# Output projection of a hybrid block by one level of Strassen's algorithm, with later left factors and accumulating transfers

## The chip, the cores and the metric

The kernel runs on one core of a Trainium2 chip, in one launch. The time is that of one execution on the device, in microseconds (us). The core has TensorE for matrix products (PE in the profile, PEld for its weight loads), VectorE (DVE), ScalarE (ACT), GpSimd (POOL) and SyncE (SP). Sixteen DMA engines carry the transfers of all queues; SP's queue for loads and POOL's software queue (q0 in the profile) matter here.

## The reference

The input `x` is 512 frames of 1024 features in float32. A layer normalises it, projects it with `w_in`, runs three branches (gated linear attention, forgetting attention, attention to memory tokens), and merges them. The part that the change touches comes after the branches:

```python
merged = gt[:, :, 0] * y_gla + gt[:, :, 1] * y_fox + gt[:, :, 2] * y_mem
h = h + merged @ w_out[l]                      # output projection, 512 x 1024 by 1024 x 1024

u2 = rmsnorm(h, g_ffn[l])
h = h + jnp.square(jax.nn.relu(u2 @ w_ff1[l])) @ w_ff2[l]    # MLP, 1024 -> 4096 -> 1024
return rmsnorm(h, g_final)
```

## The kernel before

**Matrix products.** Operands are split into a high and a low part, and each product is three matmuls (`mm3`, L159 to 162): high by high, then the two mixed ones. Weights arrive in chunks of 128 x 1024 numbers (512 KB): SP loads a chunk into `raw` (three buffers), ACT makes the high part (`whi`, L151), VectorE the low part (`wlo`, L152), with three buffers each. A chunk feeds 12 matmuls of 512 columns (24 of 256 in the MLP's first product).

**Branches and merge.** `branch` runs one of the three gated branches over eight tiles of features (`acc`, 128 features by 512 tokens). In the last branch each finished tile is halved and split into `mh` and `ml`, the left factors of the output projection.

**Output projection.** Two runs of four chunks, one per half of the output columns. Each run makes all four token tiles, `res_evac` adds a finished tile to the residual `hN[t]` (`h` in the profile) and squares it; after the second run it makes the normalised tile `un`. The second run has buffers of its own (`fhi`, `flo`) and takes the token tiles in the order 2, 3, 0, 1. `u2_turn(t)` transposes `un` of a tile on TensorE (L877) and makes the left factors of the MLP's first product for it; the turns of tiles 2, 3 and 0 are woven into the run, the turn of tile 1 follows two half products of the MLP.

**The MLP.** The 4096 hidden features are taken in four quarters `q`. In each, both products (`ff1`, `ff2`) use one level of Strassen's algorithm: an operand is cut into 2 x 2 blocks, seven products of blocks replace eight, and the factors and results are sums and differences of blocks. Left factors of `ff2` are made in `ff1_evac` behind products 7 and 3 of `ff1`. In `ff2`, products 1 and 5 stay in PSUM over the quarters, 6 and 7 are collected in `R6` and `R7`, and `evac` adds all to `hN` with VectorE; in the last quarter one of three corrections goes by an accumulating transfer from POOL (L1038).

**The sums of weights.** The right factors of the Strassen products that are sums of blocks (`T1` to `T4` for `F`, which is `w_ff1`, and `B`, which is `w_ff2`, in each quarter) are made in DRAM: a copy of one block, then transfers that add another block to it, 1 MB each. `sum_ops` lists these 64 transfers, and `next_sum` issues one on POOL's queue after each chunk's ACT cast, from the ninth cast on (`SUM_FROM = 8`). L143 is a copy, L141 an accumulating transfer.

**What sets the order.** TensorE runs in the order in which the program is written. The instructions of other engines are put in order by a scheduler ahead of time; each engine then runs its list in that order, and POOL's transfers leave through one queue in theirs.

Of the kernel before, what the change touches and what calls it, by code (L numbers as in the profile page):

```python
# [17 lines left out]
P = 128  # L18
D = 1024
# [13 lines left out]
def chunk_list():  # L33

    L = []
    L += [("T", "w_mem_kv", P * j) for j in range(4)]
    L += [("N", "w_mem_kv", 2 * j, 512) for j in range(4)]
    L += [("G",)]
    L += [("T", "w_in", OFF["fq"]), ("T", "w_in", OFF["fk"])]
    L += [("N", "w_in", 2 * j, OFF["fv"]) for j in range(4)]  # L40
    for j in range(1, 4):
        L += [("T", "w_in", OFF["fq"] + P * j), ("T", "w_in", OFF["fk"] + P * j)]
    for n, c in (("gk", 2), ("gq", 2)):
        L += [("T", "w_in", OFF[n] + P * j) for j in range(c)]
# [12 lines left out]
    return L  # L57
# [3 lines left out]
def hybrid_block(ctx, tc, chunks, wst, xT, memT, xN, cols, gffn, gfin, wup, cst, out):  # L61
# [43 lines left out]
    def load_w(key, eng=None):  # L105
# [6 lines left out]

    tsum = {(kind, n, q): dram.tile([2, P, 1024], F32, name=f"T{kind}{n}_{q}") for kind in "FB" for n in (1, 2, 3, 4)
            for q in range(4)}

# [16 lines left out]
    chunk_n = [0]  # L132
# [454 lines left out]
    def branch(gate, wo, oh, ol, n, last=None):  # L587
# [6 lines left out]
        for j in range(KT):  # L594
# [239 lines left out]
    with pool("outp") as op_:  # L834
        mh = op_.tile([P, KT, S], F32R, name="mh")
        ml = op_.tile([P, KT, S], F32R, name="ml")
        for t in range(NT):
            nc.sync.dma_start(hN[t], xN[t * P:(t + 1) * P, :])
        run(branch("gate_gla", "w_gla_o", ogh, ogl, 2, last=(mh, ml)))
        mst.close()  # L840
        oqst = ExitStack()
        oq = oqst.enter_context(pool("outq"))

        def res_evac(c):
            def go(t, ps):
                cs = slice(512 * c, 512 * c + 512)
                nc.vector.tensor_tensor(hN[t][:, cs], hN[t][:, cs], ps, op=ALU.add)
                sumsq(oq.tile([P, 512], F32, tag="hsq", name=nm("hsq"), bufs=2), hN[t], t, c, c)
                if c == 1:
                    r = rms_tile(oq, t)  # L850
                    un[t] = oq.tile([P, D], F32, tag="un", name=nm("un"), bufs=2)
                    for g in range(2):
                        gs_ = slice(512 * g, 512 * g + 512)
                        nc.vector.scalar_tensor_tensor(un[t][:, gs_], hN[t][:, gs_], r, gf[:, gs_], op0=ALU.mult, op1=ALU.mult)
            return go

        un = {}

        def own_w(key):
            hi, lo = (oq.tile([P, 1024], F32R, tag=g, name=nm(g), bufs=4) for g in ("fhi", "flo"))  # L860
            split(hi, lo, load_w(key))
            return hi, lo
# [45 lines left out]
        def load_b(kind, q, n, i):  # L908
            load_n[0] += 1
            own = kind == "B" and load_n[0] % 4 == 0  # L910
            raw = (yp if own else wp).tile([P, 1024], F32, tag="raw", name=nm("raw"))
# [10 lines left out]

        run(islice(c1, 16))
# [19 lines left out]
    with pool("ff") as yp:  # L943
# [20 lines left out]
        def ff1_evac(n, i, ps):  # L964
# [12 lines left out]
            if n == 7:  # L977
# [37 lines left out]

        def C(i, j, t):
            return hN[2 * i + t][:, 512 * j:512 * j + 512]

        def add(to, x, op=ALU.add):
            nc.vector.tensor_tensor(to, to, x, op=op)  # L1020
# [34 lines left out]
        def ff2(q):  # L1055
            for n in (1, 4, 5, 6, 7, 2, 3):
                keep = n in (1, 5)
# [24 lines left out]
def layout(inputs):  # L1082
# [7 lines left out]
    for i, c in enumerate(chunks):  # L1090
        if c[0] == "T":
            wst[i] = W[c[1]][:, c[2]:c[2] + P].reshape(KT, P, P).transpose(1, 0, 2).reshape(P, -1)
        elif c[0] == "N":
            wst[i] = W[c[1]][c[2] * P:(c[2] + 2) * P, c[3]:c[3] + 512].reshape(2, P, 512).transpose(1, 0, 2).reshape(P, -1)
        elif c[0] == "B":
            _, q, h, (kh, ch) = c
            j = 8 * q + 4 * h + int(kh) - 1
            cs = slice(512 * (int(ch) - 1), 512 * int(ch))
            for n in range(2):
                wst[i, :, 512 * n:512 * n + 512] = W["w_ff2"][(j + 2 * n) * P:(j + 2 * n + 1) * P, cs]  # L1100
        elif c[0] == "F":
# [65 lines left out]
```

## Time and profile before

| | |
|---|---|
| median of 3 runs | 865.1 us (864.47 to 867.61) |
| the profiled execution | 863.14 us, its span 861.4 us |
| PE busy | 834.2 us, 97% of the span |
| DVE / ACT / POOL busy | 558.4 / 440.1 / 95.5 us |
| output projection begins (PE) | 476.40 us |
| second product of the MLP begins (PE) | 533.70 us |

Rows of the timeline give the start in us, the duration in us, engine, line, operation, the tiles as out<-in, their shapes, how many instructions the row groups, and in brackets the idle time of the engine ahead of the row with what ended it. `mm` and `a` are PSUM tiles. In rows of groups the two numbers behind the bar are the busy time in us and the mean of one in ns. Rows by window give the length and then for PE, PEld, DVE, ACT and POOL the busy time and number, the granted clock, the share of the DMA engines and GB/s. Rows of transfers give the KB of each and the us from issue to landing. Rows of queues give packets, MB and the share of the 16 engines' time.

### The profile page before, as it was taken

How to read it: one execution, taken by the hardware profiler on the slowest of the kernel's cores; microseconds unless marked ns; L12 is line 12 of the kernel's file. 1: busy time of each engine (PE TensorE's matmuls, PEld its weight loads, DVE VectorE, ACT ScalarE, POOL GpSimd, SP SyncE). 2: the span in 40 equal slices, each digit the busy share in tenths (PEclk: the TensorE clock that was granted, in tenths of full speed). 3: DMA queues.
4: the chain of work that ended last, by engine and by line, in shares of the span. 5: the costliest groups of instructions: out<-in, count | busy, mean ns of one | idle time of the engine just before them, and what ended most of it. 6: DMA issues, size and time to landing. Idle time of an engine off the chain costs nothing. (4 is left out here: it accounts for less than half of the span.)

```text
span 861.4 us, 12076 instructions
## 1 busy us (share of the span) xinstructions
PE 834.2 (97%) x4609; PEld 711.7 (83%) x4609; DVE 558.4 (65%) x886; ACT 440.1 (51%) x704; POOL 95.5 (11%) x124
## 2 busy tenths in 40 slices
PE   7999999999999999999999998999999999999994
PEld 5778788888888888787888878997998899789973
DVE  6783756756444546474543358697579749965997
ACT  8764746754323432321332245685468448636843
POOL 5100011000101022322323200000000000000001
PEclk9999999999999999999999999999999999999998
DMA  8447789967959866699899933555554655565553
GB/s 322 143 159 255 282 204 221 215 253 188 283 192 243 315 220 186 149 221 278 294 251 342 252 128 123 172 171 196 196 174 158 218 185 175 180 208 179 172 170 117
DMA packets 39306, 180.66 MB, mean 210 GB/s; under 512 B 5040, under 2 KB 5840, under 8 KB 34640
## 3 DMA queue, kind: packets, MB, share of 16 engines
q1 hardware_dynamic: 31536, 109.09, 35.8%
q0 software_dynamic: 5920, 67.64, 30.9%
q10 hardware_dynamic: 1792, 3.16, 1.1%
q8 instruction: 36, 0.59, 0.3%
q14 instruction: 22, 0.18, 0.1%
HBM read 177.23 MB, written 69.22 MB: 286 GB/s over the span
## 5 line engine op out<-in xcount | busy, mean ns | idle before, releaser
L152 DVE TENSOR_TENSOR wlo<-raw,whi 128x1024 fp32r<-128x1024 f32 x186 | 231.8, 1248 | 163.3 <-ACT whi L151 162.8
L151 ACT CAST whi<-raw 128x1024 fp32r<-128x1024 f32 x186 | 195.3, 1051 | 240.5 <-PE mm L161 140.7
L160 PE MATMUL mm<-uhi,whi 128*128 128x512 f32 x360 | 142.5, 396 | 0.0
L161 PE MATMUL mm<-ulo,whi 128*128 128x512 f32 x360 | 140.7, 391 | 1.4 <-DVE ulo L213 1.4
L162 PE MATMUL mm<-uhi,wlo 128*128 128x512 f32 x360 | 140.5, 390 | 0.0
L161 PEld LDWEIGHTS mm<-ulo,whi 128*128 128x128 f32 x360 | 67.7, 188 | 15.7 <-DVE ulo L213 2.9
L162 PEld LDWEIGHTS mm<-uhi,wlo 128*128 128x128 f32 x360 | 67.6, 188 | 14.6 <-DVE wlo L152 0.4
L160 PEld LDWEIGHTS mm<-uhi,whi 128*128 128x128 f32 x360 | 67.7, 188 | 13.5 <-issue 0.7
L160 PE MATMUL mm<-u2h,whi 128*128 128x256 f32 x256 | 73.5, 287 | 1.5 <-ACT p L969 1.5
L162 PE MATMUL mm<-u2h,wlo 128*128 128x256 f32 x256 | 73.1, 286 | 0.0
L161 PE MATMUL mm<-u2l,whi 128*128 128x256 f32 x256 | 73.1, 286 | 0.0
L161 PE MATMUL mm<-wlo,ch 128*128 128x512 f32 x160 | 62.5, 391 | 0.7 <-DVE wlo L152 0.7
L162 PE MATMUL mm<-whi,cl 128*128 128x512 f32 x160 | 62.3, 389 | 0.0
L160 PE MATMUL mm<-whi,ch 128*128 128x512 f32 x160 | 62.3, 389 | 0.0
L161 PE MATMUL mm<-u2sl,whi 128*128 128x256 f32 x192 | 54.4, 283 | 0.0
L162 PE MATMUL mm<-u2sh,wlo 128*128 128x256 f32 x192 | 54.4, 283 | 0.0
L160 PE MATMUL mm<-u2sh,whi 128*128 128x256 f32 x192 | 54.3, 283 | 0.0
L160 PEld LDWEIGHTS mm<-u2h,whi 128*128 128x128 f32 x256 | 49.8, 195 | 1.9 <-ACT p L969 1.8
L161 PEld LDWEIGHTS mm<-u2l,whi 128*128 128x128 f32 x256 | 49.9, 195 | 0.1
L162 PEld LDWEIGHTS mm<-u2h,wlo 128*128 128x128 f32 x256 | 49.8, 195 | 0.0
L160 PEld LDWEIGHTS mm<-u2sh,whi 128*128 128x128 f32 x192 | 36.9, 192 | 0.0
L161 PEld LDWEIGHTS mm<-u2sl,whi 128*128 128x128 f32 x192 | 36.9, 192 | 0.0
(325 smaller groups left out, 1670.9 us busy)
## 6 DMA issues: line engine op xcount, KB each, us to landing
raw<-in_wst_dram SPq DMA_DIRECT2D x128, 512.0 KB, 5.9
TF<-in_wst_dram POOLq DMA_DIRECT2D x16, 1024.0 KB, 11.4
TB<-in_wst_dram POOLq DMA_DIRECT2D x16, 1024.0 KB, 11.2
raw<-TF SPq DMA_DIRECT2D x32, 512.0 KB, 4.2
raw<-TB SPq DMA_DIRECT2D x32, 512.0 KB, 3.2
xr<-in_xT_dram SPq DMA_DIRECT2D x4, 512.0 KB, 8.1
nFb<-dF ACTq DMA_DIRECT2D x8, 256.0 KB, 6.4
h<-in_xN_dram SPq DMA_DIRECT2D x4, 512.0 KB, 7.9
```

The costliest lines, as they stand in the source:

```text
L151: cast = nc.scalar.copy(hi, raw)
L152: nc.vector.tensor_tensor(lo, raw, f(hi), op=ALU.subtract)
L160: nc.tensor.matmul(ps, lh, rh, start=start, stop=False)
L161: nc.tensor.matmul(ps, lh, rl, start=False, stop=False)
L162: nc.tensor.matmul(ps, ll, rh, start=False, stop=stop)
```

## The change

- **Output projection by seven products.** `w_out` is stored in blocks like a quarter of `w_ff2` (kind `W`). Products 1, 4, 5, 6, 7, 2, 3 run in this order, each of two chunks: 14 loads where 8 were. Four of the seven right factors are sums, made in DRAM as the others are.
- **Left factors.** `merged` takes `acc` tiles in pairs, forms the differences on VectorE and splits seven slots into `mh` and `ml`, during the last branch.
- **Results.** Product 1 is copied to `E` and added to `h` by two transfers of 256 KB on POOL's queue. Behind product 6, `E` and `G` are formed on VectorE, and six transfers of 256 KB add them to `h`. The other products are added by VectorE.
- **Sums of weights.** 72 transfers instead of 64, from the fifth cast on, in three parts. The last is paced by the eighth chunk of the output projection, before by the fourth.
- **End of the projection.** Tile 0 of product 3, turns 2 and 3, tile 1 of product 3, half of the MLP's first product, turn 0, its other half, turn 1.
- **Second product of the MLP.** `late` makes the left factors S2, S3, A12 and S4 one product ahead of their use. In the last quarter product 1 goes through an ACT copy and a transfer, and all six corrections go by transfers.

```diff
-    for c in range(2):
-        L += [("N", "w_out", 2 * j, 512 * c) for j in range(4)]
+    L += [("W", 0, i, b) for b in ("11", "21", "12", "22") for i in range(2)]
...
+    quarters = [("W", 0)] + [(kind, q) for q in range(4) for kind in "FB"]
+    tsum = {(kind, n, q): dram.tile([2, P, 1024], F32, name=f"T{kind}{n}_{q}") for kind, q in quarters for n in (1, 2, 3, 4)}
...
-        for qs in ((0, 1), (2, 3)):
+        for part in (quarters[:3], quarters[3:6], quarters[6:]):
             for ops in rounds:
                 for n, src, add in ops:
-                    for q in qs:
-                        for kind in "FB":
-                            yield tsum[kind, n, q], block(kind, q, src) if isinstance(src, str) else tsum[kind, src, q], add
+                    for kind, q in part:
+                        yield tsum[kind, n, q], block(kind, q, src) if isinstance(src, str) else tsum[kind, src, q], add
...
-    SUM_FROM = 8
+    SUM_FROM = 4
...
-            if last is not None:
-                h, l = last
-                nc.scalar.mul(h[:, j, :], acc[j], 0.5)
-                nc.vector.scalar_tensor_tensor(l[:, j, :], acc[j], 0.5, f(h[:, j, :]), op0=ALU.mult, op1=ALU.subtract)
+            if last is not None and j % 2:
+                last(j // 2, acc[j - 1], acc[j])
...
+        MERGED = {1: 0, 2: 1, 4: 2, 6: 3, 7: 4, 3: 5, 5: 6}
+        mh, ml = (op_.tile([P, 4, 7, 256], F32R, name=n) for n in ("mh", "ml"))
+
+        def merged(p, e, o):
+            def to(slots, src):
+                h, l = (x[:, p, slots, :].rearrange("p s t -> p (s t)") for x in (mh, ml))
+                nc.scalar.mul(h, src, 0.5)
+                nc.vector.scalar_tensor_tensor(l, src, 0.5, f(h), op0=ALU.mult, op1=ALU.subtract)
+
+            a, b = slice(0, 256), slice(256, 512)
+            to(slice(0, 1), e[:, a])
+            to(slice(1, 3), o)
+            for dst, x, y in ((o[:, b], e[:, b], o[:, b]), (e[:, b], e[:, a], e[:, b]), (e[:, a], e[:, a], o[:, b]),
+                              (o[:, a], o[:, a], e[:, a])):
+                nc.vector.tensor_tensor(dst, x, y, op=ALU.subtract)
+            to(slice(3, 5), e)
+            to(slice(5, 7), o)
...
-        def out_w(key):
-            return own_w(key) if key[2] < 4 else get_w(key)
-
-        run(gN([("N", "w_out", 2 * j, 0) for j in range(4)], of(mh, ml), NT, at_, res_evac(0)))
-        c1 = gN([("N", "w_out", 2 * j, 512) for j in range(4)], of(mh, ml), NT, mmt, res_evac(1), tail=4, get=out_w, order=(2, 3, 0, 1))
+        def C(i, j, t):
...
+        EG = [[oq.tile([P, 512], F32, name=f"{n}{t}") for t in range(2)] for n in "EG"]
...
+        def out_evac(n, t, ps):
+            if n == 1:
+                nc.scalar.copy(EG[0][t], ps)
+                nc.gpsimd.dma_start(C(0, 0, t), EG[0][t], accum_op=ALU.add)
+            if n == 4:
+                add(C(1, 0, t), ps)
+            if n == 6:
+                E, G = EG[0][t], EG[1][t]
+                add(E, ps, ALU.subtract)
+                nc.vector.tensor_tensor(G, wps[5][t], E, op=ALU.subtract)
+                for to, x in ((C(1, 0, t), E), (C(1, 1, t), G), (C(0, 1, t), G)):
+                    nc.gpsimd.dma_start(to, x, accum_op=ALU.add)
+            if n == 7:
+                add(C(1, 0, t), ps)
+                square(2 + t, 0, 0)
+                add(C(1, 1, t), ps, ALU.subtract)
+                square(2 + t, 1, 1)
+            if n == 2:
+                add(C(0, 0, t), ps)
+                square(t, 0, 0)
+            if n == 3:
+                add(C(0, 1, t), ps)
+                square(t, 1, 1)
+        wps = {}
+        def out_mm(n, steps):
+            wps[n] = [(at_ if n == 5 else mmt)() for _ in range(2)]
+            for js in steps:
+                w = {i: [x.rearrange("p (k c) -> p k c", k=2) for x in load_b("W", 0, n, i)] for i in js}
+                for t in range(2):
+                    for i in js:
+                        for k in range(2):
+                            a, b = (x[:, 2 * i + k, MERGED[n], t * P:(t + 1) * P] for x in (mh, ml))
+                            mm3(wps[n][t], a, b, w[i][0][:, k, :], w[i][1][:, k, :], i == k == 0, i == k == 1)
+                    if js[-1] == 1:
+                        out_evac(n, t, wps[n][t])
+                    yield
+        for n in (1, 4, 5, 6, 7, 2):
+            run(out_mm(n, [[0], [1]]))
+        p3 = out_mm(3, [[0, 1]])
+        next(p3)
         u2_turn(2)
-        run(islice(c1, 8))
         u2_turn(3)
-        run(c1)
+        run(p3)
+        first = [mmt([P, 2, 256]) for _ in range(2)]
+        ff1_mm(first[0], 0, 5, 0)
         u2_turn(0)
-        first = [mmt([P, 2, 256]) for _ in range(2)]
-        for i in range(2):
-            ff1_mm(first[i], 0, 5, i)
+        ff1_mm(first[1], 0, 5, 1)
         u2_turn(1)
...
                 left(i, S1, c22[i])
-                sub(p1[i], c11[i], p1[i])
-                left(i, S3, p1[i])
-                sub(c11[i], c11[i], c22[i])
-                left(i, S2, c11[i])
             if n == 3:
                 add(p5[i], ps)
                 relu2(p5[i], p5[i])
-                left(i, A12, p5[i])
-                sub(p5[i], p5[i], c11[i])
-                left(i, S4, p5[i])
+        def late(n):
+            for i in range(2):
+                if n == 6:
+                    sub(c22[i], c11[i], c22[i])
+                    left(i, S2, c22[i])
+                if n == 7:
+                    sub(p1[i], c11[i], p1[i])
+                    left(i, S3, p1[i])
+                if n == 2:
+                    left(i, A12, p5[i])
+                if n == 3:
+                    sub(p5[i], p5[i], c22[i])
+                    left(i, S4, p5[i])
...
             if n == 1:
-                add(C(0, 0, t), ps)
+                nc.scalar.copy(p4[t], ps)
+                nc.gpsimd.dma_start(C(0, 0, t), p4[t], accum_op=ALU.add)
...
-                nc.gpsimd.dma_start(C(0, 1, t), G, accum_op=ALU.add)
-                add(C(1, 0, t), E)
-                add(C(1, 1, t), G)
+                for to, x in ((C(1, 0, t), E), (C(1, 1, t), G), (C(0, 1, t), G)):
+                    nc.gpsimd.dma_start(to, x, accum_op=ALU.add)
...
-            for n in (1, 4, 5, 6, 7, 2, 3):
+            order = (1, 4, 5, 6, 7, 2, 3)
+            for at, n in enumerate(order):
+                if at >= 2 and at < 6:
+                    late(order[at + 1])
```

On POOL, from the last tiles of the merge to the end of the projection, before (`acc<-acc,th` is a tile of the merge; `TF` and `TB` are sums of `w_ff1` and `w_ff2`):

```order
L143 DMA TB_3_107<-TB_3_99 16x16384
L141 DMA TF_2_90<-in_wst_dram 128x2048
L608 TENSOR_TENSOR acc_2104<-acc_2104,th_4076 128x512
L141 DMA TB_2_106<-in_wst_dram 128x2048
L608 TENSOR_TENSOR acc_2105<-acc_2105,th_4134 128x512
L141 DMA TF_3_91<-in_wst_dram 128x2048
L141 DMA TB_3_107<-in_wst_dram 128x2048
```

And now, where L139 is the accumulating transfer and L141 the copy (`E` and `G` are the tiles of corrections; `h_3702` to `h_3705` the four token tiles):

```order
L139 DMA TB_3_109<-in_wst_dram 128x2048
L606 TENSOR_TENSOR acc_2113<-acc_2113,th_4164 128x512
L141 DMA TB_2_103<-TB_2_101 16x16384
L141 DMA TF_3_107<-TF_3_105 16x16384
L141 DMA TB_3_111<-TB_3_109 16x16384
L139 DMA TB_2_103<-in_wst_dram 128x2048
L933 DMA h_3702<-E_4199 128x512
L933 DMA h_3703<-E_4200 128x512
L139 DMA TF_3_107<-in_wst_dram 128x2048
L139 DMA TB_3_111<-in_wst_dram 128x2048
L941 DMA h_3704<-E_4199 128x512
L941 DMA h_3705<-E_4200 128x512
```

Three copies and three accumulating transfers, with two transfers of `E` among them, now follow the last tile of the merge, and the transfers of product 6 follow those; four more of `G` come behind the last row.

On VectorE in the projection, before, from the eighth weight chunk's low half on (`hss` and `ms` are sums of squares):

```order
L152 TENSOR_TENSOR wlo_4530<-raw_4527,whi_4529 128x1024
L816 TENSOR_SCALAR hss_3698<-hss_3698 128x1
L847 TENSOR_TENSOR h_3696<-h_3696,mm_4307 128x512
L821 TENSOR_SCALAR ms_4360<-hss_3698 128x1
L854 SCALAR_TENSOR_TENSOR un_4364<-h_3696,rr_4361,gf 128x512 x2
L847 TENSOR_TENSOR h_3697<-h_3697,mm_4308 128x512
```

And now, from the eighth of fourteen on:

```order
L150 TENSOR_TENSOR wlo_4355<-raw_4352,whi_4354 128x1024
L863 TENSOR_TENSOR E_4199<-E_4199,mm_4331 128x512
L150 TENSOR_TENSOR wlo_4386<-raw_4383,whi_4385 128x1024
L863 TENSOR_TENSOR E_4200<-E_4200,mm_4332 128x512
L939 TENSOR_TENSOR G_4201<-a_4291,E_4199 128x512
L939 TENSOR_TENSOR G_4202<-a_4292,E_4200 128x512
L150 TENSOR_TENSOR wlo_4404<-raw_4401,whi_4403 128x1024
L863 TENSOR_TENSOR h_3704<-h_3704,mm_4381 128x512
L150 TENSOR_TENSOR wlo_4452<-raw_4449,whi_4451 128x1024
L812 TENSOR_SCALAR hss_3706<-hss_3706 128x1
L863 TENSOR_TENSOR h_3705<-h_3705,mm_4382 128x512
L150 TENSOR_TENSOR wlo_4470<-raw_4467,whi_4469 128x1024
```

The low half of the ninth chunk (`wlo_4386`) now stands behind the subtraction from `E_4199`, which overwrites what a transfer of product 1 reads; that of the eleventh (`wlo_4452`) stands behind the add of product 7 to `h_3704`, which comes after a transfer of product 6 into the same place.

On VectorE where the MLP's second product begins in a quarter, before (`c`, `p` and `cl` are tiles of hidden features and the low parts of left factors):

```order
L152 TENSOR_TENSOR wlo_793_5161<-raw_791_5158,whi_792_5160 128x1024
L955 TENSOR_TENSOR c111_4617<-c111_4617,c221_4619 128x512
L213 TENSOR_TENSOR cl0_4628<-c110_4616,ch0_4626 128x512
L213 TENSOR_TENSOR cl1_4629<-p51_4623,ch1_4627 128x512
L955 TENSOR_TENSOR p50_4622<-p50_4622,c110_4616 128x512
L1020 TENSOR_TENSOR h2_3696<-h2_3696,mm_781_5116 128x512
L213 TENSOR_TENSOR cl1_4629<-p11_4621,ch1_4627 128x512
L152 TENSOR_TENSOR wlo_796_5179<-raw_794_5176,whi_795_5178 128x1024
```

And now:

```order
L150 TENSOR_TENSOR wlo_817_5227<-raw_815_5224,whi_816_5226 128x1024
L211 TENSOR_TENSOR cl1_4711<-p51_4705,ch1_4709 128x512
L211 TENSOR_TENSOR cl1_4711<-p11_4703,ch1_4709 128x512
L1004 TENSOR_TENSOR p50_4704<-p50_4704,c220_4700 128x512
L863 TENSOR_TENSOR h2_3704<-h2_3704,mm_805_5176 128x512
L1004 TENSOR_TENSOR c221_4701<-c111_4699,c221_4701 128x512
L150 TENSOR_TENSOR wlo_820_5245<-raw_818_5242,whi_819_5244 128x1024
```

Between these two low halves stand five operations where six were.

More of the change, by code (lines that the diff above doesn't have):

```diff
@@ L109, in load_w @@
         return raw
-    tsum = {(kind, n, q): dram.tile([2, P, 1024], F32, name=f"T{kind}{n}_{q}") for kind in "FB" for n in (1, 2, 3, 4)
-            for q in range(4)}
+    quarters = [("W", 0)] + [(kind, q) for q in range(4) for kind in "FB"]
+    tsum = {(kind, n, q): dram.tile([2, P, 1024], F32, name=f"T{kind}{n}_{q}") for kind, q in quarters for n in (1, 2, 3, 4)}
     def block(kind, q, b):
@@ L834, in hybrid_block @@
     with pool("outp") as op_:
-        mh = op_.tile([P, KT, S], F32R, name="mh")
-        ml = op_.tile([P, KT, S], F32R, name="ml")
+        MERGED = {1: 0, 2: 1, 4: 2, 6: 3, 7: 4, 3: 5, 5: 6}
[13 more added lines that the diff above has]
+            to(slice(5, 7), o)
         for t in range(NT):
             nc.sync.dma_start(hN[t], xN[t * P:(t + 1) * P, :])
-        run(branch("gate_gla", "w_gla_o", ogh, ogl, 2, last=(mh, ml)))
+        run(branch("gate_gla", "w_gla_o", ogh, ogl, 2, last=merged))
         mst.close()
@@ L842, in hybrid_block, with add, square @@
         oq = oqst.enter_context(pool("outq"))
[L844 to L855, printed above, removed]
-        un = {}
[L859 to L862, printed above, removed]
-        def out_w(key):
-            return own_w(key) if key[2] < 4 else get_w(key)
-        run(gN([("N", "w_out", 2 * j, 0) for j in range(4)], of(mh, ml), NT, at_, res_evac(0)))
-        c1 = gN([("N", "w_out", 2 * j, 512) for j in range(4)], of(mh, ml), NT, mmt, res_evac(1), tail=4, get=out_w, order=(2, 3, 0, 1))
+        un = {}
+        def C(i, j, t):
+            return hN[2 * i + t][:, 512 * j:512 * j + 512]
+        def add(to, x, op=ALU.add):
+            nc.vector.tensor_tensor(to, to, x, op=op)
+        def square(t, c, n):
+            sumsq(oq.tile([P, 512], F32, tag="hsq", name=nm("hsq"), bufs=2), hN[t], t, c, n)
+            if n == 1:
+                r = rms_tile(oq, t)
+                un[t] = oq.tile([P, D], F32, tag="un", name=nm("un"), bufs=2)
+                for g in range(2):
+                    gs_ = slice(512 * g, 512 * g + 512)
+                    nc.vector.scalar_tensor_tensor(un[t][:, gs_], hN[t][:, gs_], r, gf[:, gs_], op0=ALU.mult, op1=ALU.mult)
+        EG = [[oq.tile([P, 512], F32, name=f"{n}{t}") for t in range(2)] for n in "EG"]
         a21, s1 = (oq.tile([P, 4, 256], F32, name=n) for n in ("a21", "s1"))
@@ L909, in load_b @@
             load_n[0] += 1
-            own = kind == "B" and load_n[0] % 4 == 0
+            own = kind != "W" and load_n[0] % 4 == 0 and not (kind == "F" and q == 0)
             raw = (yp if own else wp).tile([P, 1024], F32, tag="raw", name=nm("raw"))
@@ L921, in ff1_mm @@
                     mm3(ps[:, a, :], wh[:, a, k, :], wl[:, a, k, :], uh[:, k, :], ul[:, k, :], k == 0, k == 3)
-        run(islice(c1, 16))
+        def out_evac(n, t, ps):
+            if n == 1:
+                nc.scalar.copy(EG[0][t], ps)
[36 more added lines that the diff above has]
+        next(p3)
         u2_turn(2)
-        run(islice(c1, 8))
         u2_turn(3)
-        run(c1)
+        run(p3)
+        first = [mmt([P, 2, 256]) for _ in range(2)]
+        ff1_mm(first[0], 0, 5, 0)
         u2_turn(0)
-        first = [mmt([P, 2, 256]) for _ in range(2)]
-        for i in range(2):
-            ff1_mm(first[i], 0, 5, i)
+        ff1_mm(first[1], 0, 5, 1)
         u2_turn(1)
```

8 lines of the change are left out of this document (2 added, 6 removed).

## Prediction

> **What bounds the kernel now.** I read the page's busy shares first, then the 40 slices, then the PE timeline of the output projection.
>
> ```profile
> span 861.4 us, 12076 instructions
> PE 834.2 (97%) x4609; PEld 711.7 (83%) x4609; DVE 558.4 (65%) x886; ACT 440.1 (51%) x704; POOL 95.5 (11%) x124
> PE   7999999999999999999999998999999999999994
> PEclk9999999999999999999999999999999999999998
> DMA  8447789967959866699899933555554655565553
> ```
>
> TensorE is busy 97% of the span at full clock, so matmuls are the bound nearly everywhere, and only removed matmuls or removed waits can help. The DMA engines are the other full resource: eights and nines in slices 18 to 23 (366 to 495 us), of which the last is the first half of the output projection. Its matmuls, row by row:
>
> ```profile
> 476.40 0.39 PE L160 MATMUL a<-whi,mh 128*128 128x512 f32 x1
> 476.62 0.39 PE L161 MATMUL a<-wlo,mh 128*128 128x512 f32 x1
> 510.56 1.32 PE L877 MATMUL a<-cst_s,un 128*128 128x128 f32 x8 [1.36 <-DVE un L854]
> 524.31 0.36 PE L160 MATMUL mm<-u2h,whi 128*128 128x256 f32 x1
> 530.03 0.28 PE L162 MATMUL mm<-u2h,wlo 128*128 128x256 f32 x1
> 532.66 1.29 PE L877 MATMUL a<-cst_s,un 128*128 128x128 f32 x8 [2.35 <-DVE un L854]
> 533.70 0.36 PE L160 MATMUL mm<-u2h,whi 128*128 128x256 f32 x1
> 534.98 0.41 PE L161 MATMUL mm<-u2l,whi 128*128 128x256 f32 x1
> 535.19 0.42 PE L162 MATMUL mm<-u2h,wlo 128*128 128x256 f32 x1
> ```
>
> Durations overlap in the pipeline; the price of a matmul is the step between starts: 0.225 us for 512 columns (476.40 to 476.62; 0.227 over longer stretches), and 5.72/47 = 0.12 us for 256 (48 matmuls start from 524.31 to 530.03). The projection starts at 476.40, and the second product of the MLP's first quarter at 533.70. Between them are 192 matmuls x 0.227 = 43.6 us, four turns (transposes of one token tile) of 1.03 us (532.66 to 533.70) = 4.1, 48 x 0.12 = 5.8 us of the MLP's first product, and waits of 1.4 and 2.4: 57.3 us, all accounted for. After the second wait matmuls of 256 columns step by 0.21 instead of 0.12 (534.98 to 535.19), until 537.5; that slower clock costs about 1.6 more.
>
> **The matmuls removed.** Seven products of 24 matmuls replace 192: 168. Gain 24 x 0.227 = 5.4 us. The new end order has a half product between the last turns, so both waits (3.8) and the slow stretch (1.6) can go too. If nothing is late, the projection takes 168 x 0.227 + 4.1 + 5.8 = 48.0 us and the second product starts at 524.4, against an effective 535.3: **-10.8 us**.
>
> **The added work beside it.** Six more weight chunks are split, and the left factors of the projection are formed during the merge.
>
> ```profile
> L152 DVE TENSOR_TENSOR wlo<-raw,whi 128x1024 fp32r<-128x1024 f32 x186 | 231.8, 1248 | 163.3 <-ACT whi L151 162.8
> 440.00:460.00 20.00, 20.00 (x90) 16.57 (x89) 7.09 (x7) 5.83 (x8) 4.36 (x5) 1.00 1.02 314
> ```
>
> A chunk feeds 12 matmuls = 2.72 us, and DVE needs 1.25 for its split: covered by half. In the merge (second row: length, then PE, PEld, DVE busy) DVE works 7.1 of 20 us, so the left factors (3.8 us per pair of tiles by those counts, 1.4 before) fit. Both cost 0 while transfers keep up; uncovered, a factor pair would cost 2.4. Two ACT copies of product 1 are hidden too (ACT is busy 51%). The six more loads on SP's queue go into the next part.
>
> **The transfers, which decide it.** The sums of weight quarters that the MLP uses later are built by 1 MB transfers, all on POOL's one software queue (q0), one per weight chunk cast. Before, the last of them is issued at the fourth chunk of the projection. After, there are 72, and the last goes with the eighth. Behind sums in that same queue now stand eight 256 KB accumulating transfers: two of product 1, six of product 6. VectorE waits for these.
>
> ```profile
> 466.88 0.84 POOL L141 DMA_DIRECT2D TF<-in_wst_dram  x1 [1.65 <-ACT whi L151]
> 475.00 0.83 POOL L141 DMA_DIRECT2D TB<-in_wst_dram  x1 [4.38 <-ACT whi L151]
> TF<-in_wst_dram POOLq DMA_DIRECT2D x1, 1024.0 KB, 11.4
> ...
> q0 software_dynamic: 1099, 8.09, 73.4%
> q1 hardware_dynamic: 1036, 3.79, 17.0%
> TF<-in_wst_dram POOLq DMA_DIRECT2D x4, 1024.0 KB, 11.6
> raw<-in_wst_dram SPq DMA_DIRECT2D x8, 512.0 KB, 9.7
> ...
> q0 software_dynamic: 256, 8.39, 44.9%
> ...
> TF<-in_wst_dram POOLq DMA_DIRECT2D x1, 1024.0 KB, 8.3
> ```
>
> The first row's sum is the third (issue to landing 11.4 us): it lands at 478.3. The next four rows are the DMA view of 111 to 171 us, with eight accumulates and eight loads: one accumulate takes 0.734 x 60/8 = 5.5 us of all 16 engines, one load 0.17 x 60/8 = 1.3, together 6.8. The row after them is 59 to 111, with eight plain copies: 0.449 x 52/8 = 2.9 each. Alone, an accumulate lands after 8.3 (last row). For 256 KB I take a quarter of 5.5 = 1.4; the nearest row of that size landed after 3.3, which is the other end:
>
> ```profile
> h<-c POOLq DMA_DIRECT2D x2, 256.0 KB, 3.3
> ```
>
> By the new order of POOL, the queue then is: before the sum that lands at 478.3 an accumulate stands where a copy was (+2.6: 480.9); accumulate at the second chunk (+6.8: 487.7); three copies (+8.7: 496.4); accumulate (+6.8: 503.2); the two of product 1 (+2.8: 506.0); two accumulates, beside which no load runs if PE stands (2 x 5.5: 517.0); the first of product 6 (+1.4: **518.4**), the fifth at 524.0. Ends: 514.6 with 5.5 for each accumulate and 2.5 for a copy, 528 with 3.3 for each small one and a load's 1.3 beside each copy.
>
> What waits: ideally product 7 ends at 476.4 + 10 x 2.72 = 503.6. On VectorE the add of product 7 stands behind the first of product 6's transfers, and the low half of the eleventh chunk stands behind that add; so TensorE gets it at 518.4 + 0.68 + 1.25 = 520.3. (An earlier stop, of the ninth chunk behind product 1's transfers at 506, lies inside this.) Product 2 then runs to 525.8. VectorE waits for the fifth transfer at 524.0, then adds, makes the normalised tiles and the last two low halves in its queue:
>
> ```profile
> L1020 DVE TENSOR_TENSOR h<-h,mm 128x512 f32<-128x512 f32 x24 | 15.8, 678 | 0.0
> 509.75 1.41 DVE L854 SCALAR_TENSOR_TENSOR un<-h,rr,gf 128x512 f32<-128x512 f32 x2 [0.75 <-POOL rr L822]
> ```
>
> From 525.8: add 0.68, chunk 13 1.25, small sums 0.2, tile 1.5, chunk 14 1.25 = 530.7. TensorE then has half a product tile (1.4), two turns (2.1), the other tile (2.7), half a MLP product (2.9), a turn, the other half and a turn (4.9): 544.7. That is 20.3 past the ideal 524.4, and after so long a stop I add the 1.6 of slow clock seen above: **+21.9 us** (18 to 32 by the ends).
>
> The Trainium skill, page "DMA: Bandwidth & Descriptors", section "Anatomy of one DMA — SWDGE (gpsimd) path", fits such a transfer as about 2.0 us + bytes/436e3, an estimate of 2.4 us of moving for 1 MB. By that the queue would be empty near 500 and nothing would wait. The trace's 5.5 us of all engines per accumulate disagrees; the page describes no accumulating transfer between two DRAM places, and I go by the trace.
>
> **The MLP.** Left factors of the second product are made one product ahead instead of all in the last steps of the first, so one VectorE operation fewer stands ahead of a low half there.
>
> ```profile
> 586.30 0.50 PE L161 MATMUL a<-wlo,ch 128*128 128x512 f32 x1 [0.66 <-DVE wlo L152]
> 660.00:680.00 20.00, 19.34 (x86) 15.70 (x85) 17.93 (x23) 9.21 (x11) 0.00 (x0) 1.00 0.55 186
> 740.00:760.00 20.00, 19.34 (x86) 15.69 (x85) 17.62 (x24) 9.03 (x11) 0.00 (x0) 1.00 0.58 191
> 820.00:840.00 20.00, 19.48 (x85) 15.33 (x84) 20.00 (x27) 9.14 (x10) 0.90 (x1) 1.00 0.52 165
> ```
>
> TensorE stands about 0.5 to 0.7 at each of four boundaries; one operation of 0.68 fewer ends most of it: **-2.0** (0 to -2.6). In the last quarter eight transfers replace six VectorE adds while VectorE is busy throughout (20.00); q0 is empty there, the eight at 3.3 have the length of products 7 and 2 (10.9 us), so 0 at the end of the span, within 1 either way. The sums that start four casts earlier meet loads of 9.7 us that PE, in nines there, did not feel: 0, at most one wait like the 2.35 above.
>
> **Sum.** The profiled run took 863.1. 863.1 - 10.8 + 21.9 - 2.0 = 872.2; that run is 2.0 under the median of 865.1, so **874** against the median.
>
> **Rivals.** *Hidden* (faster): the queue drains by 503.6, fifteen us sooner than I count, and no add waits; 863.1 - 10.8 - 2.0 + 2.0 = 852. It decides when the first transfer of product 6 lands before product 7's last matmul. For it: 256 KB alone took 3.3. Against it: three quarters of the engines' time went to q0 wherever accumulates ran. The Trainium skill's fit above leads here. *Partly hidden*: engines serve q0 with most of their time, loads fall behind instead, and the landing is near 510; 874 - 8 = 866, between 855 and 868. For it: loads needed 10.5 us to land in this stage while q0 had 68%, and TensorE did not wait. *Worse*: each small transfer takes 3.3 and loads share the copies, 528: 884 and up; also if VectorE, full near the ends of the MLP, then waits for transfers there.
>
> ```profile
> q0 software_dynamic: 609, 5.24, 68.2%
> raw<-in_wst_dram SPq DMA_DIRECT2D x5, 512.0 KB, 10.5
> ```
>
> **How the numbers follow.** My forecast, a stop of TensorE of some 15 to 20 us that outweighs the matmuls saved, 0.61 (its own range 868 to 884). Hidden 0.17, partly hidden 0.13, worse 0.09. About 0.5% (4.3 us, 860.8 to 869.4) can be told from no change. Hidden and a third of partly hidden are faster: 0.22; the rest of partly hidden with the low edge of the forecast is the same: 0.12; slower 0.66. The range runs from 852, through half of the hidden case, to 888; it leaves out half of hidden (0.09) and about half of worse (0.05).
>
> **What the changed profile would show.** Right: TensorE idle over 10 us between 498 and 525, ended by VectorE's low half of the ninth and eleventh chunks, VectorE before them idle for POOL's queue; sums landing up to 517; 168 matmuls in the projection; granted clock low after the stop. The four 0.66 waits before the second product shrink. Wrong: the small transfers land within 4 us of issue and TensorE's projection takes about 48 us; or the stop is at the loads (raw) rather than the adds; or the MLP's VectorE waits grow instead.

## The result and the profile after

The changed kernel takes 894.6 us (893.1 to 895.5), against 866.1 for the kernel before in the same measurement: 1.033 times as long, 95% interval 1.030 to 1.035. The forecast of slower was right; 874, and its upper end of 888, were too low.

The page of the changed kernel, the lines that answer to those of before:

```profile
span 892.7 us, 12148 instructions
PE 841.2 (94%) x4585; PEld 715.3 (80%) x4585; DVE 574.3 (64%) x916; ACT 450.7 (50%) x722; POOL 112.7 (13%) x146
PE   7999999999999999999999657699999999999994
PEclk8999999999999999999999869799999999999998
DMA  8487998787679888658999993445645655465574
```

There are 24 matmuls fewer (4585 for 4609), yet TensorE is busy 7 us longer. In slices 23 to 26 it has holes, and its granted clock is lower there (8, 6, 9 and 7 tenths); but for the clock of the first slice, the rest of both rows is as before. So nearly the whole loss is in the projection and the turns behind it. TensorE's timeline there, only the first matmul, the main waits, and the start of the MLP's second product (560.03):

```profile
478.46 0.39 PE L158 MATMUL mm<-whi,mh 128*128 128x512 f32 x1
...
494.94 0.80 PE L158 MATMUL a<-whi,mh 128*128 128x512 f32 x1 [5.18 <-ACT whi L149]
...
515.03 0.80 PE L159 MATMUL mm<-wlo,mh 128*128 128x512 f32 x1 [1.89 <-DVE wlo L150]
...
531.86 0.80 PE L159 MATMUL mm<-wlo,mh 128*128 128x512 f32 x1 [8.54 <-DVE wlo L150]
...
542.65 0.50 PE L159 MATMUL mm<-wlo,mh 128*128 128x512 f32 x1 [2.42 <-DVE wlo L150]
...
560.03 0.36 PE L158 MATMUL mm<-u2h,whi 128*128 128x256 f32 x1
...
572.85 0.58 PE L158 MATMUL mm<-u2h,whi 128*128 128x256 f32 x1 [6.83 <-ACT p L1018]
```

And before, where the fifth product of the MLP (the one after a wait for ACT's copies `p`) starts at 542.73:

```profile
542.73 0.39 PE L160 MATMUL mm<-u2h,whi 128*128 128x256 f32 x1 [1.55 <-ACT p L969]
```

From the first matmul of the projection to the fifth product it is 572.85 - 478.46 = 94.4 us, before 542.73 - 476.40 = 66.3: +28.1. I call this stretch the stage below. TensorE's busy time grew by 2.6 us in it, by 2.3 ahead of it and by 2.1 behind. What lies ahead of it is 2.1 longer, what lies behind 1.2 (892.7 - 572.85 = 319.8 for 861.4 - 542.73 = 318.7). Ahead of it the earlier sums and the added left factors are at work, but they cost next to nothing: in the first 60 us the granted clock was 0.94 here and 1.00 before, and in two of the traces below (corrections on VectorE, more work for VectorE), with the same program up to the projection and a clock of 1.00, the projection starts at 476.60 and 476.74, before at 476.40. At 0.91 it starts at up to 481.27. So stages are the better measure between traces. They have a spread too: in the run of the MLP part alone, where nothing of the stage was edited, it took 67.9 us for 66.3 before.

The waits on VectorE in the same place:

```profile
513.15 0.69 DVE L863 TENSOR_TENSOR E<-E,mm 128x512 f32<-128x512 f32 x1 [5.05 <-DMA h<-E]
513.76 1.22 DVE L150 TENSOR_TENSOR wlo<-raw,whi 128x1024 fp32r<-128x1024 f32 x1
...
529.98 0.69 DVE L863 TENSOR_TENSOR h<-h,mm 128x512 f32<-128x512 f32 x1 [11.18 <-DMA h<-E]
530.59 1.22 DVE L150 TENSOR_TENSOR wlo<-raw,whi 128x1024 fp32r<-128x1024 f32 x1
```

These are the two operations that the prediction named (the first is the subtraction from `E`), each with the low half of a chunk behind it, the ninth and the eleventh. POOL's and ACT's timelines show where the sums stood:

```profile
485.91 0.50 POOL L141 DMA_DIRECT2D TF<-TF  x1 [3.53 <-ACT whi L149]
495.17 0.49 POOL L141 DMA_DIRECT2D TB<-TB  x1 [8.76 <-ACT whi L149]
497.56 0.85 POOL L139 DMA_DIRECT2D TB<-in_wst_dram  x1 [1.90 <-ACT whi L149]
498.11 2.11 POOL L933 DMA_DIRECT2D h<-E  x2
499.47 1.61 POOL L139 DMA_DIRECT2D TF<-in_wst_dram  x1
507.14 0.81 POOL L139 DMA_DIRECT2D TB<-in_wst_dram  x1 [6.05 <-ACT whi L149]
514.14 0.87 POOL L941 DMA_DIRECT2D h<-E  x1 [6.20 <-DVE E L863]
```

```profile
493.84 1.04 ACT L149 CAST whi<-raw 128x1024 fp32r<-128x1024 f32 x1 [8.23 <-DMA raw<-TW]
```

And the DMA view of 468 to 490 us:

```profile
q0 software_dynamic: 454, 4.19, 80.7%
q1 hardware_dynamic: 536, 1.99, 23.7%
...
raw<-TW SPq DMA_DIRECT2D x4, 512.0 KB, 13.4
...
TB<-TB POOLq DMA_DIRECT2D x1, 10.3
TF<-TF POOLq DMA_DIRECT2D x1, 8.8
```

The sums hold 81% of the engines' time, a chunk needs 13.4 us to land, ACT's cast waits 8.2 us for one, and POOL's next sum waits for that cast. The loop closes: sums make chunks late, and late chunks make the last sums late. The last one is issued at 507.14, the first small transfer of product 6 behind it at 514.14, and the add runs at 529.98.

### The profile page after: what moved, and what is told of

The parts are those of the page before. It is cut to its first block, busy times and chain, and to the rows that moved or that the text cites. A ratio compares the mean times of both kernels' runs of the same rounds, so it can differ in the third digit from the quotient of the medians.

```text
span 892.7 us, 12148 instructions
## 1 busy us (share of the span) xinstructions
PE 841.2 (94%) x4585; PEld 715.3 (80%) x4585; DVE 574.3 (64%) x916; ACT 450.7 (50%) x722; POOL 112.7 (13%) x146
## 5 line engine op out<-in xcount | busy, mean ns | idle before, releaser
L150 DVE TENSOR_TENSOR wlo<-raw,whi 128x1024 fp32r<-128x1024 f32 x194 | 241.5, 1247 | 175.1 <-ACT whi L149 170.4
L149 ACT CAST whi<-raw 128x1024 fp32r<-128x1024 f32 x194 | 203.7, 1051 | 269.6 <-PE mm L159 137.8
```

The lines of the kernel that those rows point to most:

```text
L149: cast = nc.scalar.copy(hi, raw)
L150: nc.vector.tensor_tensor(lo, raw, f(hi), op=ALU.subtract)
```

## The experiments

Theory A: VectorE waits for small transfers that stand behind sums in one queue. Theory B: the sums take the DMA engines from the chunks. Theory C, later D: the end of the projection is limited by VectorE's own work, whatever the transfers do.

**No sum in the projection.** The last eight sums come later, one per three chunks, in the MLP's first quarter.

```diff
+        if paused[0]:
+            paused[0] += 1
+            if paused[0] < 17 or paused[0] % 3:
+                return
         chunk_n[0] += 1
...
+        paused[0] = 1
         wps = {}
```

(The last edit stands ahead of the projection's first chunk.)

> The changed kernel, but no weight chunk of the projection paces a sum: the last eight sums come later, one per three chunks, in the MLP's first quarter. Theory A (the eight small transfers stand behind the sums in POOL's queue, and VectorE behind them) and theory B (the sums take the DMA engines, so that TensorE lacks chunks) both expect the stops between 487 and 545 us gone, the MLP's second product near 526 instead of 560. Theory C (the turns, put close together at the end, pile up work on VectorE and ACT) expects the wait of 6.8 us ahead of the MLP's fifth product to stay: total 858 to 862. If that wait is only a consequence of the stops: 852 to 856. Rival: later sums starve the MLP's loads instead, 865 or more.

Measured: 875.5 us (872.7 to 878.6), 19 less than the changed kernel.

```profile
480.11 0.39 PE L164 MATMUL mm<-whi,mh 128*128 128x512 f32 x1
...
550.99 0.58 PE L164 MATMUL mm<-u2h,whi 128*128 128x256 f32 x1 [8.42 <-ACT p L1025]
```

The stage is 70.9 us instead of 94.4, and no wait of TensorE is left in it before 513. So the sums' place is the cause of most of the loss (A and B together). The second product still starts only at 536.6, where A and B expected 526. The wait ahead of the fifth product stayed, 8.4 us, which speaks for C; the total is above C's 858 to 862. Part of the excess lies in the MLP: 876.8 - 550.99 = 325.8 us behind the stage, 7.1 more than before, where the later sums now compete with the MLP's chunks. That is the rival named, here beside the others. Its price is not fixed: with the same later sums, the five traces of kernels below take 319.7 to 326.6 us there.

**Corrections on VectorE, sums in place.**

```diff
-                nc.gpsimd.dma_start(C(0, 0, t), EG[0][t], accum_op=ALU.add)
+                add(C(0, 0, t), EG[0][t])
...
-                    nc.gpsimd.dma_start(to, x, accum_op=ALU.add)
+                    add(to, x)
```

> The changed kernel, but the eight corrections of the projection are added by VectorE (eight more adds of 0.68 us), the sums stay where they are. Theory A expects the stop of 8.5 us and most of the others gone, 10 to 18 us faster than the changed kernel: 877 to 884. Theory B expects chunks to stay late and little gain: 886 to 892. Rival: eight adds overload VectorE: no gain or worse.

Measured: 883.1 us (881.9 to 884.0), 11.5 less than the changed kernel; the stage, from 476.60 on, 85.3. That is in A's range, but most of the loss is left:

```profile
494.79 0.79 PE L158 MATMUL a<-whi,mh 128*128 128x512 f32 x1 [5.54 <-ACT whi L149]
...
561.91 0.58 PE L158 MATMUL mm<-u2h,whi 128*128 128x256 f32 x1 [6.96 <-ACT p L1018]
```

The wait for a chunk (5.5 us) is there as in the changed kernel. A and B both hold: of 28 us, 9 go without the small transfers alone, 23.5 without the sums alone.

**The MLP part alone**, on the kernel before (the diff's edits to `ff1_evac`, `evac`, `ff2` and `own`).

> The kernel before with the MLP part of the change alone (later left factors, last corrections by transfers, own load buffers for F). The prediction's term: -2.0 us against before (0 to -2.6). If the last corrections by transfers cost at the end: 0 or slower.

Measured: 863.5 us, 0.9964 of before (0.9943 to 0.9985). Behind its fifth product the trace takes 862.1 - 546.02 = 316.1 us, 2.6 less than before. The term of -2.0 was right, and the transfers of the last quarter cost nothing at the end: from the start of the last matmul to the end of the span it took 11.0 us, before 11.5.

**Both edits**, no sum in the projection and corrections on VectorE.

> Both edits: no sum paced in the projection, and the eight corrections on VectorE. If a transfer of 256 KB delays VectorE even with an empty queue (3.3 us from issue to landing in the trace of before), this is 2 to 5 us faster than the pause alone; if VectorE is what is full at the end of the projection, it is up to 5 us slower.

Measured: 869.9 us (867.4 to 875.1), 5.6 less than the pause alone: a transfer of 256 KB delays VectorE even with an empty queue, a little more than expected. The other expectation, up to 5 us slower with a full VectorE, was not met: eight adds cost less than the waits for transfers that they replace. Now no transfer disturbs the projection, and this is the run from which C can be read:

```profile
481.27 0.39 PE L164 MATMUL mm<-whi,mh 128*128 128x512 f32 x1
...
519.98 3.46 PE L890 MATMUL a<-cst_s,un 128*128 128x128 f32 x16 [2.74 <-DVE un L878]
...
547.60 0.58 PE L164 MATMUL mm<-u2h,whi 128*128 128x256 f32 x1 [5.45 <-ACT p L1025]
```

The stage is 66.3 us, that of before. Seven products instead of eight, undisturbed by transfers, gain nothing here. Two windows of this kernel, its whole stage and the end of it (length, then PE, PEld, DVE, ACT, POOL busy):

```profile
481.27:547.60 66.33, 56.21 (x297) 47.70 (x295) 58.80 (x87) 36.45 (x58) 6.25 (x7) 0.95 0.62 184
502.00:547.00 45.00, 35.48 (x206) 30.52 (x204) 43.07 (x67) 24.78 (x44) 3.92 (x6) 0.93 0.62 183
```

VectorE works 43.1 of the last 45 us while TensorE, with waits and a clock of 0.93, works 35.5. Over the stage of the kernel before, VectorE worked 41.1 us where it is 58.8 now, and TensorE 61.0 where it is 56.2:

```profile
476.40:542.73 66.33, 61.03 (x322) 52.24 (x320) 41.09 (x61) 28.81 (x48) 6.10 (x7) 0.97 0.56 159
```

So while TensorE was relieved, VectorE was loaded: with six more splits, the last differences of the merge, and here the eight corrections.

**More work for VectorE**: the normalised tiles are written twice.

```diff
-                    nc.vector.scalar_tensor_tensor(un[t][:, gs_], hN[t][:, gs_], r, gf[:, gs_], op0=ALU.mult, op1=ALU.mult)
+                    for _ in range(2):
+                        nc.vector.scalar_tensor_tensor(un[t][:, gs_], hN[t][:, gs_], r, gf[:, gs_], op0=ALU.mult, op1=ALU.mult)
```

> The kernel with the pause and VectorE corrections (869.9), but VectorE writes each normalised tile twice: eight more operations of 0.7 us, 5.6 in all, between 510 and 540 us. Theory D (VectorE is full from the end of product 6 to the MLP's fifth product and bounds this stretch): 4.5 to 6 slower, 874 to 876. Rival (TensorE's waits there come from the order and latency of the turns, VectorE has room): 0 to 2 slower.

Measured: 876.4 us (869.5 to 878.3), 6.5 more than its base; in the trace the stage is 546.90 - 476.74 = 70.2, 3.8 more, and VectorE's busy time in it 63.5, 4.7 more. D by the stage; the median is a weaker witness, since the executions spread and the trace is of the shortest.

**Turns further apart.**

```diff
+        u2_turn(2)
         p3 = out_mm(3, [[0, 1]])
         next(p3)
-        u2_turn(2)
         u2_turn(3)
```

> The same base, but the turn of tile 2 stands ahead of product 3 and that of tile 3 between its two tiles, so that the turns lie further apart on TensorE. Theory D: the same within 2 us, since VectorE's work is the same. Rival (order of the turns): 4 to 8 faster.

Measured: 873.4 us (869.0 to 876.3), 3.5 more; the stage 547.10 - 478.98 = 68.1, 1.8 more. The order is no remedy, and the rival's 4 to 8 less is out: the turn of tile 2 waited 5.9 us for its tile. D's "same within 2" holds for the stage, not for the median.

**Work from VectorE to POOL**, adds and low halves of chunks.

```diff
-                add(C(0, 0, t), EG[0][t])
+                nc.gpsimd.tensor_tensor(C(0, 0, t), C(0, 0, t), EG[0][t], op=ALU.add)
...
+            return split_w(raw, nc.gpsimd if i == 0 and ((kind == 'W' and n in (7, 2, 3)) or (kind == 'F' and q == 0 and n in (5, 4, 1))) else None)
```

> The same base, but POOL takes work from VectorE: the four adds into the first two token tiles that are needed last, and six low halves of chunks (the first chunk of products 7, 2, 3 and of three half products of the MLP), about 9.8 us of VectorE. Theory D: 5 to 9 faster, 861 to 865. Rival: POOL is slow (1.28 to 2.33 us for 128x512 in the trace of before) and TensorE waits for its low halves: 870 or more.

Measured: 878.0 us, 8 more than its base, in the rival's range. In its trace POOL needs 2485 ns for a low half where VectorE needs 1248, the stage is 72.4 us, and the wait ahead of the fifth product grew:

```profile
L156 POOL TENSOR_TENSOR wlo<-raw,whi 128x1024 fp32r<-128x1024 f32 x6 | 14.9, 2485 | 21.4 <-ACT whi L155 21.4
...
508.19 4.55 DVE L869 TENSOR_TENSOR h<-h,G 128x512 f32<-128x512 f32 x2
...
552.93 0.58 PE L164 MATMUL mm<-u2h,whi 128*128 128x256 f32 x1 [10.59 <-ACT p L1026]
```

No wait of TensorE in the stage is put down to a low half on POOL. What the trace does show: the loads of chunks waited 5.4 us for POOL's low halves to leave `raw`, and VectorE was slower beside POOL's work (the two adds of the second row took 4.55 us, where all four of them take 2.49 in its base). So VectorE's busy time fell only from 58.8 to 56.9, not by 9.8, and for or against D the run says nothing.

**Low parts of the turns on POOL**, where nobody waits for them soon.

```diff
-                to(S2, sub(s1[:, :, sl], pts[0], s1[:, :, sl]))
-                to(S3, sub(a21[:, :, sl], pts[0], a21[:, :, sl]))
+                sub(s1[:, :, sl], pts[0], s1[:, :, sl])
+                sub(a21[:, :, sl], pts[0], a21[:, :, sl])
...
+                to(S2, s1[:, :, sl], nc.gpsimd)
+                to(S3, a21[:, :, sl], nc.gpsimd)
+                to(S4, s4, nc.gpsimd)
```

> The same base, but in turns 0 and 1 VectorE forms the three differences first and POOL makes their low parts: 3.7 us off VectorE, and the ACT casts of the differences no longer wait for a late VectorE operation. Theory D: 3 to 4 faster, 866 to 867. If the wait of 5.5 us ahead of the fifth product is only ACT's order (casts that wait for VectorE stand ahead of the PSUM copies): 5 to 7 faster.

Measured: 867.7 us (861.3 to 871.9), 2.2 less than its base; the stage is 541.15 - 477.92 = 63.2, 3.1 less, about as much as VectorE was relieved (55.5 us busy in it for 58.8). The wait ahead of the fifth product fell from 5.45 to 2.57. That this is VectorE's load and not ACT's order of casts is not settled by it, since the edit changes both. Behind the stage this trace took 326.6 us, ten more than the MLP part alone.

**Later sums at longer distance.**

```diff
-            if paused[0] < 17 or paused[0] % 3:
+            if paused[0] < 20 or paused[0] % 5:
```

> The kernel whose turns leave low parts to POOL, with the eight later sums one per five chunks instead of three. After the fifth product it took 326.6 us of its trace where the kernel with the MLP part alone took 316.1. If the later sums starve the MLP's loads: 3 to 7 faster, 861 to 865. If the longer MLP comes from a slow clock after the stop: no change, 867 to 869.

Measured: 866.6 us (861.7 to 870.2), in neither forecast; behind the stage 321.4 us, 5.2 less in the trace, 1.2 in the median, which is within the spread. By all traces the later sums do cost in the MLP: with them it takes 319.7 to 326.6 us behind the stage, in the three kernels below without them 316.7 to 318.9.

**The last eight sums earlier**, in the kernel with the low parts on POOL.

```diff
-        op = next(sums, None) if chunk_n[0] > SUM_FROM else None
-        if op is not None:
+        for _ in range((chunk_n[0] > SUM_FROM) + (chunk_n[0] in (26, 31, 36, 41, 46, 50, 54, 58))):
+            op = next(sums, None)
+            if op is None:
+                break
```

> The same kernel, but the last eight sums are issued earlier, as a second transfer at eight chunks between the 26th and the 58th, so none is left for the projection or the MLP. If DMA engines have room there (shares of 0.69 to 0.85 between 180 and 420 us): projection and MLP run free, 858 to 864. If not, loads are late in the branches: 868 or more.

Measured: 862.0 us (860.3 to 864.7), 0.9952 of before (0.9930 to 0.9973): faster than both kernels. The stage is 63.1 us and what follows it 316.7, the least of any with the new projection.

```profile
478.72 0.39 PE L166 MATMUL mm<-whi,mh 128*128 128x512 f32 x1
...
541.84 0.39 PE L166 MATMUL mm<-u2h,whi 128*128 128x256 f32 x1 [2.56 <-ACT p L1031]
```

**The changed kernel with that one edit.**

> The changed kernel with one edit: its last eight sums are issued earlier, as in the kernel before this one, so that the eight small transfers of the projection meet an empty queue. If the sums in the projection are the cause of the stops: 22 to 26 us faster than the changed kernel, 868 to 872. What is then left against the kernel of 861.95 is its small transfers with an empty queue (4.6 us by the pause) and the low parts on VectorE (3.1). If the transfers cost nothing with an empty queue: 863 to 866.

Measured: 868.5 us (865.3 to 872.2), 26 less than the changed kernel, 1.002 of before (1.000 to 1.004). The stage is 548.80 - 478.74 = 70.1. One table of eight chunk numbers takes back nearly all of the loss, with every transfer of the change in place.

**The same with corrections on VectorE.**

> The same with the eight corrections of the projection on VectorE. It differs from the kernel of 861.95 only by the low parts of turns 0 and 1, made by VectorE here. Theory D (VectorE bounds the end of the projection): 3.1 slower than that kernel, 864 to 866. Else the same, 861 to 863.

Measured: 867.0 us (864.6 to 869.3), 5.0 more than the kernel of 862.0, in the trace a stage of 544.36 - 477.03 = 67.3 for 63.1. The only difference is some 3 us of VectorE's work (58.6 us busy in the stage for 55.6) and ACT's order. It is in line with D, a little more than expected. Against the run before it, the median is 1.5 less and the stage 2.7: that is what the small transfers cost with an empty queue here, less than the 5.6 of the first pair.

Six traces have the new projection with no transfer in VectorE's way (both edits, more work, turns further apart, low parts on POOL, sums earlier, and this one). VectorE's busy time in their stages goes from 55.5 to 63.5 us, and the stage is 6.7 to 9.3 us longer than that in each (25 us longer in the kernel before), while ACT's is 36.2 to 36.5 in all. That speaks for D.

## Why the prediction was right and wrong

**Matmuls removed, right; the gain of 10.8, wrong.** 24 matmuls are gone. What failed here is the step "The new end order has a half product between the last turns, so both waits (3.8) and the slow stretch (1.6) can go too": the ideal was made with TensorE alone, and "the added work beside it" was priced per chunk (1.25 in 2.72) and for the merge, not for the end of the projection. There adds, normalised tiles, turns and splits fill VectorE (43.1 of 45 us), and with no transfer in the way the stage is 66.3 us instead of the 55.5 that the ideal gives: the second product starts 54.9 us after the first matmul (536.16 - 481.27), not 48.0, and a wait follows. The gain was nil; 3.2 us came with some of VectorE's work on POOL. In the forecast itself this error cancels, since +21.9 is counted from the same ideal's end, 524.4: the sum stands on the landing below and on what follows it.

**The transfers, right in mechanism, too small in size; here the sum failed.** The places were as named: the ninth and eleventh chunks behind operations that wait for POOL's queue. The step that failed is the first landing of product 6: 518.4 predicted, 529.98 measured for the add behind it. The projection began 2.1 later than before, so that this is 51.5 us after its first matmul for 42.0 in the sum: 9.5 late, as late as the upper end of 528. Three parts make it up:

- 4.2: the queue was taken as always full. Its third copy was issued at 495.17, after the two ahead of it had landed (481.84 + 10.3 = 492.1 and 485.91 + 8.8 = 494.7), since the cast that paces it waited for a chunk; the three copies ended at 502.7, not 496.4 (with the 2.1, 498.5).
- 1.0: the sum behind them, issued at 497.56, landed 12.9 us later, at 510.5.
- 4.3: from there two small ones, two sums and the first of product 6 took 19.5 us, for 15.2 in the sum, which took no load to run beside the two sums. Loads did run, with 24.2% of the engines' time, 4.7 us of the 19.5 (first row below, 510 to 530 us); without them the prices per transfer held.

The prediction had loads falling behind as a rival that makes it milder. They made it worse, because casts pace the sums; and the stop at 494.94 is at a load, which the prediction had listed as a sign of being wrong.

```profile
q1 hardware_dynamic: 508, 1.81, 24.2%
...
TB<-in_wst_dram POOLq DMA_DIRECT2D x1, 1024.0 KB, 12.9
...
TB<-TB POOLq DMA_DIRECT2D x1, 7.5
```

(The other rows are of the transfers issued at 497.56 and at 495.17.) From the eleventh chunk's low half to the second product, the prediction had 544.7 - 520.3 = 24.4 us; it took 560.03 - 531.8 = 28.2, at a granted clock of 0.73 between 520 and 540: 3.8 more. In all, the trace missed the 872.2 of the sum by 22.3 us (894.5): 2.1 ahead of the projection, 9.5 and 3.8 here, 3.8 from the second to the fifth product (12.8 for 9.0), and 3.2 behind it (1.2 more than before, where 2.0 less was forecast).

**The wait ahead of the fifth product was not foreseen.** 6.83 us for 1.55, and behind it matmuls that step by 0.21 us instead of 0.12 until 578.4:

```profile
573.45 0.41 PE L160 MATMUL mm<-u2h,wlo 128*128 128x256 f32 x1
573.66 0.41 PE L158 MATMUL mm<-u2h,whi 128*128 128x256 f32 x1
...
578.54 0.28 PE L160 MATMUL mm<-u2h,wlo 128*128 128x256 f32 x1
578.66 0.28 PE L158 MATMUL mm<-u2h,whi 128*128 128x256 f32 x1
```

It is the end of the stretch that VectorE fills: ACT's casts of differences wait for VectorE, and the copies `p` that free PSUM stand behind them.

```profile
571.69 0.62 ACT L210 CAST u2sh<-s 128x512 fp32r<-128x512 f32 x1 [4.14 <-DVE s L893]
572.22 2.04 ACT L1018 COPY p<-mm 128x512 f32<-128x512 f32 x4
```

**The MLP, right**: -2.6 by the run of this part alone, for -2.0; in the changed kernel 24 steps of 0.21 us behind the wait above hide it (24 x 0.09 = 2.2 us). **The end of the span and the earlier sums, right**: from the last matmul to the end the changed kernel took 12.3 us for 11.5 before, inside the 1 either way, and the earlier sums cost 0.2 to 0.3 by the two traces with the clock of before.

**The rule of the page on transfers** (the Trainium skill, "DMA: Bandwidth & Descriptors", section "Anatomy of one DMA — SWDGE (gpsimd) path"): by its fit nothing would wait. The trace's 5.5 us of all engines for an accumulating transfer of 1 MB was the price to go by, and the fit's estimate of 2.4 us of moving is not borne out for such a transfer by any run here.

**The chances.** Slower had 0.66, and "worse", 884 and up, which came true, 0.09: its landing at 528 was met, though in part by a queue that ran empty, which it did not name. The range of the likeliest case counted the queue's uncertainty and not a second bound behind it.

Put together, against the stage of before: with the sums and small transfers away 0 to 1 (66.3 and 67.3, where -10.8 was expected), with the small transfers alone put back 3.7 to 4.5 (70.1 and 70.9), with the sums put back too 28.1.

## What to carry to other kernels

Where products are saved, sum the other engines' work over the stretch that gets shorter: the work that was beside the saved matmuls stays, and the next engine may already be full. In this kernel a transfer on whose landing an engine waits must not share a queue with background transfers, and background work paced by the foreground slows itself and what it is paced by; place it where the DMA view of the trace shows room. Eight numbers did that here, worth 26 us.

## What was not expected of the hardware

A low half on POOL took 2485 ns where VectorE took 1248 with the same shapes, and VectorE itself was slower beside POOL's work. In the kernel with the turns' low parts on POOL, one of VectorE's low halves took 4.99 us while POOL made three low parts:

```profile
539.88 4.99 DVE L156 TENSOR_TENSOR wlo<-raw,whi 128x1024 fp32r<-128x1024 f32 x1
```

Software transfers held 81% of the DMA engines' time against chunks' 24%, and chunks of 512 KB landed after 13.4 us, though three of them could be under way. The MLP's chunks after the pause landed in 7 to 10 us, and in 3.3 in the changed kernel with the earlier sums, where no software transfer ran:

```profile
raw<-TB SPq DMA_DIRECT2D x8, 512.0 KB, 10.1
raw<-in_wst_dram SPq DMA_DIRECT2D x8, 512.0 KB, 7.1
...
raw<-TB SPq DMA_DIRECT2D x7, 512.0 KB, 3.3
```

(550 to 620 us; the first two rows are of the kernel with the pause.) What stays open is how much of the wait ahead of the fifth product is VectorE's load and how much ACT's order, and so whether VectorE's load alone bounds the end of the projection.
